# Moving the block products from the second batch to the first, in a two-branch sequence layer

## The chip, the cores and the metric

The kernel runs on one core of one Trainium2 chip. The metric is the device time of one execution in microseconds (us). The core has a matrix engine (TensorE, PE in the profile, with its weight loads as PEld), VectorE (DVE), ScalarE (ACT), GpSimd (POOL) and SyncE (SP), which here only issues DMAs. SBUF is the on-chip memory that all of them read; PSUM holds what TensorE writes.

## What is computed

One layer is applied to two batches (1024 positions, 1024 channels each) with the same weights. All data is float32. Cut to what matters:

```python
xn = rmsnorm(x, g_pre)
p = xn @ w_in
fv, fg, hv, hg, mg = jnp.split(p, [1024, 2048, 5120, 6144], axis=-1)

fz = jnp.fft.fftn(fv.reshape(B, L, 4, 256), axes=(1, 3), norm="ortho").real
y_f = (fz.reshape(B, L, 1024) * jax.nn.silu(fg)) @ w_fourier_out

hv = short_conv(hv, w_short)              # width 3 over the sequence
v, x1, x2 = jnp.split(hv, 3, axis=-1)
kf = hyena_filters(...)                   # same for both batches
z = v
for n, gate in enumerate((x1, x2)):
    z = gate * long_conv(z, kf[:, n], hyena_d[n])
y_h = (z * jax.nn.silu(hg)) @ w_hyena_out

g_f, g_h = jnp.split(jax.nn.sigmoid(mg + b_merge), 2, axis=-1)
out = (g_f * y_f + g_h * y_h) @ w_out
return x + rmsnorm(out, g_post)
```

The code numbers the in-projection's sections of 1024 columns, the Fourier input left out: 0 is fg, 1 to 3 are v, x1 and x2 ahead of the short convolution, 4 is hg, 5 and 6 are the two merge gates. A section has eight column tiles of 128 channels; with seven sections that is 56 tiles for each batch.

## The kernel before

To keep float32 accuracy, every large product is made three times over: each operand is split into a rounded high part and a low rest (`split`, L167: ScalarE rounds, another engine subtracts), and TensorE adds high x high, high x low and low x high (`mm3`, L467). A plain column tile (`inproj`, L836) is 8 row tiles x 3 x 2 halves of 512 positions, 48 matmuls of 512 columns. The split of its weights (wh and wl, from wr) has its subtraction on POOL.

A pair of column tiles can also be made by products of 2 x 2 blocks (`times`, L1101, used in `phase_gates`): seven products of block sums in place of eight, 84 matmuls in place of 96. This needs sums of row blocks (`sums`, L1110: xsum, th and tl), made once for a batch, and sums of weight blocks for each pair (`prepare`, L1129: wraw, wsum and their splits).

The stages follow each other: `phase_fourier` (both batches' norm and Fourier branch, stored in DRAM), `phase_main`, `phase_gates`, `phase_out` (output products). `phase_main` first makes the 16 filter spectra (2 orders x 8 channel tiles): taps, sums of absolute values (acc), butterflies (xp, xm, b) and a small transform (pXf), stored as kt. Beside them TensorE works on plain tiles of the first batch (`spill_gate`, L873). Then `branches` (L1030) runs 32 convolution steps, for each batch 2 orders x 8 channel tiles. A step transposes folded inputs (`conv_front`: eo, tph, xt), makes a butterfly (b, split into bh and bl), transforms (pX), multiplies by the spectrum (t, Y, split into yh and yl), transforms back (pT) and gates the result (`gate`). The steps of the two orders alternate, and the front of a step is issued ahead of the back of the one before. Beside the steps, `conv` (L863) makes the tile of v, x1 or x2 that a step needs: a plain in-projection, then three taps read from PSUM, one on ScalarE and two on VectorE. The first batch also stores its split weights in DRAM (d_w), and the second reads them there. The rows of the batch in work (xh and xl) are loaded and split by `load_x` (L823), ahead of each batch.

The tile framework assigns buffers and lets each instruction wait for its operands. It orders the instructions of every engine ahead of time; each engine then works through its own list in that order.

What the second batch gets before the change: its 24 tiles of v, x1 and x2 plain, 10 gate tiles plain near the end of the convolutions (`PLAIN`, L1116), and its other 22 gate tiles as 11 pairs of block products in `phase_gates`. The first batch's 56 tiles are all plain.

Of the kernel before, what the change touches and what calls it, by code (L numbers as in the profile page):

```python
# [9 lines left out]
F32 = mybir.dt.float32  # L10
# [127 lines left out]
NH = 6  # L138
NF = 8
# [6 lines left out]
GROUPS = [(0, (0, 1)), (2, (4, 5)), (1, (2, 3)), (3, (6, 7))]  # L146
KOFF = {0: 0, 1: 8, 2: 16, 3: 24}
# [13 lines left out]
class K:  # L161
# [34 lines left out]
    def setup(self, ctx):  # L196
# [28 lines left out]
        self.d_w = [[[dt(f"d_w{s}_{k}_{i}", [P, L]) for i in range(2)] for k in range(8)] for s in range(3)]  # L225
# [430 lines left out]
    def butterfly(self, ws, xp, xm):  # L656
# [77 lines left out]
    def filter_taps(self, n, ct, rates, ws):  # L734
# [8 lines left out]
        for m in range(4):  # L743
# [11 lines left out]
            if m:  # L755
                self.add("dve", accf, accf, ex)
# [14 lines left out]
    def filter_spectrum(self, n, ct, T, ws):  # L771
# [64 lines left out]
    def inproj(self, sec, mt, b=None):  # L836
# [3 lines left out]
        for q in range(2):  # L840
            s = slice(512 * q, 512 * q + 512)
            h = self.wp.tile([P, 4, P], F32R, tag="wh", name="wh", bufs=3)
            l = self.wp.tile([P, 4, P], F32R, tag="wl", name="wl", bufs=3)
            parts = [t.rearrange("p a b -> p (a b)") for t in (h, l)]
            kept = self.d_w[sec - 1][mt] if b is not None else None
            if b:
                for t, k in zip(parts, kept):
                    nc.sync.dma_start(t.bitcast(F32), k[:, s])
            else:
                r = self.wp.tile([P, 512], F32, tag="w", name="wr", bufs=2)  # L850
                nc.sync.dma_start(r, a["w_in"][sec, mt][:, s])
                self.split(*parts, r, "pool", "act")
                if kept:
                    for t, k in zip(parts, kept):
                        nc.gpsimd.dma_start(k[:, s], t.bitcast(F32))
# [7 lines left out]
    def conv(self, sec, ct, ws, name, b):  # L863
        nc = self.nc
        ps = self.inproj(sec, ct, b)
        out = ws.tile([P, L], F32, tag="u" if sec == 1 else "x", name=name, bufs=1 if sec == 1 else 4)
        w = lambda j: self.wsh[:, ((sec - 1) * 8 + ct) * 3 + j:((sec - 1) * 8 + ct) * 3 + j + 1]
        nc.scalar.activation(out, ps, AF.Copy, scale=w(1))
        self.stt("dve", out[:, 1:L], ps[:, 0:L - 1], w(0), out[:, 1:L])
        self.stt("dve", out[:, 0:L - 1], ps[:, 1:L], w(2), out[:, 0:L - 1])  # L870
        return out

    def spill_gate(self, b, sec, ct, ws):  # L873
# [4 lines left out]
        for n in range(2):  # L878
            s = slice(512 * n, 512 * n + 512)
            t = self.wp.tile([P, 512], F32, tag="gt", name="gt", bufs=3)  # L880
            if sec:
                nc.scalar.copy(t, ps[:, s])
            else:
                f = self.wp.tile([P, 512], F32, tag="gt", name="fz", bufs=3)
                nc.sync.dma_start(f, self.d_fz[b][ct][:, s])
                nc.scalar.activation(t, ps[:, s], AF.Silu)
                self.mul("dve", t, t, f)
            nc.sync.dma_start(self.d_g[b][sec][ct][:, s], t)


    def conv_front(self, u, ws):
# [4 lines left out]
        self.sub("dve", eo[:, 1], u4[:, :, P:2 * P], u4[:, :, P - 1::-1])  # L896
# [8 lines left out]
    def conv_back(self, n, ct, B, ws):  # L905
# [3 lines left out]
        for g, pairs in GROUPS:  # L909
# [25 lines left out]
            self.split(yh, yl, Y, "dve", "act")  # L935
# [47 lines left out]
    def phase_main(self, nct=8, nb=NB, nf=16):  # L983
        tc, nc, a = self.tc, self.nc, self.a
        with ExitStack() as es:
# [4 lines left out]
            with tc.issue_after(self.fz_stored.ins):  # L990
                self.load_x(0, range(4))
# [5 lines left out]
            with tc.issue_after(self.third[0].ins), tc.issue_after(self.third[1].ins):  # L997
                nc.scalar.copy(self.hid, hid)
                self.sub("dve", self.hid[64:128], hid[64:128], self.hid[64:128])
            taps = self.filter_taps(0, 0, self.filter_rates(0, 0, ws), ws)  # L1000
            self.load_x(0, range(4, 8))
# [3 lines left out]
            nc.gpsimd.tensor_copy(self.cfwd[:, 0, 0:1], self.xl[4][:, 0:1])  # L1005
            nc.gpsimd.dma_start(self.cfwd, a["c_fwd"])
            plain = [(5, c) for c in range(8)] + [(6, c) for c in range(8)] + [(4, c) for c in range(NH)]
            fill = sorted([((2 * c + 1) / len(plain), t) for c, t in enumerate(plain)]
                          + [((2 * c + 1) / max(NF, 1), (0, c)) for c in range(NF)])
            fill = [t for _, t in fill]  # L1010
            rates = self.filter_rates(1, 0, ws)
            for i in range(nf):
                nxt = self.filter_taps((i + 1) % 2, (i + 1) // 2, rates, ws) if i + 1 < nf else None
                self.filter_spectrum(i % 2, i // 2, taps, ws)
                if i + 2 < nf:
                    rates = self.filter_rates(i % 2, i // 2 + 1, ws, self.rounded)
# [13 lines left out]
    def branches(self, nb, nct, ws):  # L1030
# [10 lines left out]
        plain = list(self.PLAIN)  # L1041
# [576 lines left out]
```

## Time and profile before

| | us |
|---|---|
| median of 3 runs | 2398.74 |
| lowest and highest run | 2398.69, 2399.79 |
| span of the profiled execution | 2394.9 |
| last plain tile of the second batch ends | 1677.1 |
| block products (pg) run from there for about | 207.5 |

The span runs from the first to the last instruction of one profiled execution; the rest of the time lies around it. Durations of single instructions come from that execution. Busy time of an engine is the time in which at least one of its instructions ran; matmuls overlap in the pipeline, so the mean duration of one matmul (391 ns) is longer than the time between two. Idle time is put down to what ended it. A windows row gives, for a stretch of the span, its length and then the busy time and the count of instructions of each engine, the granted TensorE clock as a share of full speed, the share of DMA time and the DMA rate in GB/s.

### The profile page before, as it was taken

The numbers are of one execution on the slowest core, as the hardware profiler recorded it, in microseconds if no ns is written. First come the engines' busy times: TensorE is split into PE (matmuls) and PEld (weight loads), VectorE is DVE, ScalarE is ACT, GpSimd is POOL, SyncE is SP. The second block draws the span as 40 slices with busy tenths as digits, with TensorE's granted clock in tenths as the row PEclk, the third lists the DMA queues.
The fourth block names the chain that finished last, engine by engine and source line by source line (L and its number), as shares of the span: only waits on it lengthen the run. The fifth ranks groups of instructions, "written<-read, shape, count | busy, mean of one in ns | idle before, by whom it ended". The sixth has DMA issues, their size and how long they took to land.

```text
span 2394.9 us, 36369 instructions
## 1 busy us (share of the span) xinstructions
PE 2360.9 (99%) x12988; PEld 2053.6 (86%) x12988; DVE 1889.5 (79%) x3397; ACT 1084.2 (45%) x2063; POOL 461.6 (19%) x506
## 2 busy tenths in 40 slices
PE   6999999999999999999999999999999999999998
PEld 5998888888888888888888888888888888888887
DVE  7875787888879999999989999985555456665677
ACT  6654666677643333333322223333443445444444
POOL 3341222222232233230000000023000111112111
PEclk9999999999999999999999999999999999999999
DMA  8636655555665555545444444435544667776553
GB/s 264 219 129 220 204 169 165 171 171 159 204 215 177 172 170 187 176 145 203 150 131 133 137 150 133 143 121 198 165 160 141 211 215 259 251 259 213 166 166 132
DMA packets 221007, 428.33 MB, mean 179 GB/s; under 512 B 23254, under 2 KB 80952, under 8 KB 220570
## 3 DMA queue, kind: packets, MB, share of 16 engines
q1 hardware_dynamic: 193037, 333.03, 43.1%
q0 software_dynamic: 27568, 92.94, 11.5%
q8 instruction: 102, 1.67, 0.3%
q14 instruction: 79, 0.65, 0.1%
q10 hardware_dynamic: 221, 0.04, 0.0%
HBM read 290.12 MB, written 135.79 MB: 178 GB/s over the span
## 4 chain that ended last, share of the span: by engine, by line
PE 94%; DVE 2%; DMA 1%; ACT 1%; issue 1%; POOL 0%; DVEq 0%; ACTq 0%; POOLq 0%; SPq 0%
PE pin L193 41%; PE pg L193 8%; PE pyf L193 7%; PE pyh L193 7%; PE pX L193 7%; PE pT L193 7%; PE po L193 6%; PE pXf L193 3%; PE pfv L193 3%; PE pft L193 1%; PE tph L901 1%; DVE eo L180 0%; PE pQ L193 0%; DMA wr<-in_w_fo 0%; PE pse L193 0%
## 5 line engine op out<-in xcount | busy, mean ns | idle before, releaser
L193 PE MATMUL pin<-xh,wl 128*128 128x512 f32 x1440 | 563.2, 391 | 0.0
L193 PE MATMUL pin<-xl,wh 128*128 128x512 f32 x1440 | 562.8, 391 | 0.1
L193 PE MATMUL pin<-xh,wh 128*128 128x512 f32 x1440 | 561.9, 391 | 0.0
L180 POOL TENSOR_TENSOR wl<-wr,wh 128x512 fp32r<-128x512 f32 x132 | 227.6, 1725 | 1148.7 <-ACT wh L170 1125.4
L193 PEld LDWEIGHTS pin<-xl,wh 128*128 128x128 f32 x1440 | 271.0, 188 | 50.8 <-DVE xl L180 0.4
L193 PEld LDWEIGHTS pin<-xh,wh 128*128 128x128 f32 x1440 | 270.8, 188 | 51.0
L193 PEld LDWEIGHTS pin<-xh,wl 128*128 128x128 f32 x1440 | 271.0, 188 | 50.5
L170 ACT CAST wh<-wr 128x512 fp32r<-128x512 f32 x260 | 161.1, 620 | 333.6 <-PE pin L193 107.8
L180 DVE TENSOR_TENSOR t<-pX,k 128x1024 f32<-128x1024 f32 x128 | 155.6, 1216 | 9.8 <-PE pX L193 6.5
L193 PE MATMUL pX<-bh,cfwd 128*128 128x256 f32 x768 | 162.3, 289 | 0.0
L180 DVE TENSOR_TENSOR wl<-wr,wh 128x512 fp32r<-128x512 f32 x128 | 87.9, 688 | 91.5 <-ACT wh L170 91.5
L193 PE MATMUL pyf<-sf,wh 128*128 128x512 f32 x512 | 157.7, 389 | 0.0
L193 PE MATMUL pyh<-sh,wh 128*128 128x512 f32 x512 | 157.4, 389 | 0.0
L193 PE MATMUL pT<-cinv,yh 128*128 128x256 f32 x768 | 145.3, 284 | 0.0
L193 PEld LDWEIGHTS pT<-cinv,yh 128*128 128x128 f32 x768 | 123.2, 190 | 6.8
L170 ACT CAST bh<-b 128x512 fp32r<-128x512 f32 x144 | 89.1, 620 | 87.3 <-DVE b L180 50.6
L193 PEld LDWEIGHTS pX<-bh,cfwd 128*128 128x128 f32 x768 | 126.4, 190 | 2.2
L193 PEld LDWEIGHTS pyf<-sf,wh 128*128 128x128 f32 x512 | 96.1, 188 | 20.0
L193 PEld LDWEIGHTS pyh<-sh,wh 128*128 128x128 f32 x512 | 96.1, 188 | 20.0
L193 PE MATMUL pT<-cinv,yl 128*128 128x256 f32 x384 | 109.0, 284 | 0.0
L193 PE MATMUL pX<-bl,cfwd 128*128 128x256 f32 x384 | 108.9, 284 | 0.0
L170 ACT CAST yh<-y 128x512 fp32r<-128x512 f32 x96 | 59.4, 619 | 100.9 <-DVE y L180 98.0
(384 smaller groups left out, 5340.6 us busy)
## 6 DMA issues: line engine op xcount, KB each, us to landing
k<-d_k SPq DMA_DIRECT2D x128, 512.0 KB, 4.1
wr<-in_w_in SPq DMA_DIRECT2D x132, 256.0 KB, 3.2
d_g<-gt SPq DMA_DIRECT2D x124, 256.0 KB, 2.6
d_k<-kt SPq DMA_DIRECT2D x128, 128.0 KB, 2.2
d_k<-kt SPq DMA_DIRECT2D x64, 256.0 KB, 2.3
wr<-in_w_fo POOLq DMA_DIRECT2D x64, 256.0 KB, 4.0
g<-d_g SPq DMA_DIRECT2D x64, 256.0 KB, 4.2
wr<-in_w_ho POOLq DMA_DIRECT2D x64, 256.0 KB, 3.9
```

Source lines behind the costliest of these rows:

```text
L170: self.rounded = nc.scalar.copy(h, src)
L180: return e.tensor_tensor(out, a, b, op=op)
L193: return self.nc.tensor.matmul(out, lhsT, rhs, start=start, stop=stop, skip_group_check=shared)
L901: nc.tensor.transpose(tp[:, q * P:(q + 1) * P], eo[:, e, q], self.ident)
```

## The change

The two batches swap their treatment. A new stage `phase_products` stands ahead of `phase_main` and makes the whole in-projection of the first batch: four tiles plain (`FIRST`), the other 52 as 26 pairs of block products (`JOBS`). The tiles of v, x1 and x2 get their taps there, read from SBUF, and are stored (d_v); hg is stored behind its SiLU. `phase_gates` is gone, and so are the stored split weights (d_w).

`phase_main` now loads the second batch's rows ahead of the filters, and all 56 tiles of that batch are plain: 16 beside the filters (`FILL`), 17 beside the first batch's convolutions (`SIDE`, eight of them tiles of v, x1 and x2, listed in `AHEAD`, which are stored in d_v), 16 where the second batch's steps need them, and 7 near the end (`LAST`). The first batch's steps load v, x1 and x2 from DRAM. The product with SiLU(hg) is now made in the convolution step for both batches.

Several subtractions, additions and products move from VectorE to POOL: the low parts of b and y in the convolutions and filters, the sum of absolute taps, the odd folds of the filters and of the convolution inputs, the product with SiLU(hg), and two of the splits of a block product's weights. Two copies of the butterfly become one. Filters and convolutions are given a higher priority in the ordering than the plain tiles beside them. The first operands of `phase_out` go to buffers of their own and wait for the last convolution instead of the last block product.

```diff
+OFF = 1000
...
-        def split(g, b):
+        def split(g, b, eng="pool"):
...
-            self.split(h, l, b, "dve", "act")
+            self.split(h, l, b, eng, "act")
...
-        self.sub("dve", b2[:, 2], xp[:, 1, 3], xp[:, 1, 1])
-        self.sub("dve", b2[:, 3], xp[:, 1, 0], xp[:, 1, 2])
+        self.sub("dve", b2[:, 2:4], xp[:, 1, 3::-3], xp[:, 1, 1:3])
...
-                self.add("dve", accf, accf, ex)
+                self.add("pool", accf, accf, ex)
...
-            self.sub("dve", O[:, 2 * h:2 * h + 2], t[:, :, 0], t[:, :, 1])
+            self.sub("pool", O[:, 2 * h:2 * h + 2], t[:, :, 0], t[:, :, 1])
...
-        self.sub("dve", eo[:, 1], u4[:, :, P:2 * P], u4[:, :, P - 1::-1])
+        self.sub("pool", eo[:, 1], u4[:, :, P:2 * P], u4[:, :, P - 1::-1])
...
-            self.split(yh, yl, Y, "dve", "act")
+            self.split(yh, yl, Y, "pool", "act")
...
+    def conv(self, sec, ct, ws, name, b, tag=None):
+
+        tag = tag or ("u" if sec == 1 else "x")
+        out = ws.tile([P, L], F32, tag=tag, name=name, bufs=1 if tag == "u" else 4)
+        if b == 0 or (sec, ct) in self.AHEAD and name != "ahead":
+            self.nc.sync.dma_start(out, self.d_v[b][sec][ct])
+        else:
+            self.taps(out, self.inproj(sec, ct), sec, ct)
         return out
+
+    def beside(self, sec, c, ws):
+
+        if sec in (1, 2, 3):
+            out = self.conv(sec, c, ws, "ahead", 1, "u")
+            self.nc.sync.dma_start(self.d_v[1][sec][c], out)
+        else:
+            self.spill_gate(1, sec, c, ws)
...
-            with tc.issue_after(self.fz_stored.ins):
-                self.load_x(0, range(4))
+            self.load_x(1, range(4))
...
+            self.load_x(1, range(4, 8))
+            fill = self.FILL
...
+                with tc.high_priority(OFF):
+                    nxt = self.filter_taps((i + 1) % 2, (i + 1) // 2, rates, ws) if i + 1 < nf else None
+                    self.filter_spectrum(i % 2, i // 2, taps, ws)
...
-                    self.spill_gate(0, sec, c, ws)
+                    self.spill_gate(1, sec, c, ws)
...
+            if b == 0 and i:
+                for _ in range(len(side) - 15 + i if i > 13 or len(side) > 16 - i and i > 8 else 1):
+                    self.beside(*side.pop(0), ws)
...
+                    self.mul("pool", X[i][:, s], X[i][:, s], g)
...
-                if i + 2 < len(steps) and steps[i + 2][0] != steps[i + 1][0]:
-                    self.load_x(steps[i + 2][0])
-            y = self.conv_back(n, c, B, ws)
+            with tc.high_priority(OFF):
+                y = self.conv_back(n, c, B, ws)
...
-    PLAIN = [(5, 0), (5, 1), (6, 0), (6, 1), (5, 2), (5, 3), (6, 2), (6, 3), (5, 4), (5, 5)]
-
-    def phase_gates(self):
+    FIRST = [(5, 0), (5, 1), (5, 2), (5, 3)]
+    JOBS = ([(5, c) for c in (4, 6)] + [(s, c) for c in (0, 2, 4, 6) for s in (1, 4, 2, 0, 3)]
+            + [(6, c) for c in (0, 2, 4, 6)])
+    FILL = [(5, c) for c in range(8)] + [(6, c) for c in range(8)]
+    AHEAD = [(1, 0), (2, 0), (3, 0), (3, 1), (3, 2), (3, 3), (3, 4), (3, 6)]
+    SIDE = [(4, 0), (1, 0), (4, 1), (2, 0), (4, 2), (3, 0), (4, 3), (3, 2), (4, 4), (3, 4), (4, 5), (3, 6), (4, 6), (3, 1), (4, 7), (0, 0), (3, 3)]
+    LAST = [(0, c) for c in range(1, 8)]
+
+    def phase_products(self):
...
-                parts("s4", gw, ("s4h", "s4l"), s[:, 3], 1)
-                parts("22", gw, ("a2h", "a2l"), r[:, 3], 1)
+                parts("s4", gw, ("s4h", "s4l"), s[:, 3], 1, "pool")
+                parts("22", gw, ("a2h", "a2l"), r[:, 3], 1, "pool")
...
+            with tc.high_priority(600):
+                for k in range(4):
+                    if k == 2:
+                        A = prepare(*jobs[0])
...
+                if sec in (1, 2, 3):
+                    V[c, n] = True
+                    if (c, 1 - n) in V:
+                        o = xp.tile([P, L], F32, tag=f"xl{2 + c % 2}", name="tapped", bufs=1)
+                        self.taps(o, V[c], sec, c)
+                        nc.sync.dma_start(self.d_v[b][sec][c], o)
...
-            with tc.issue_after(self.copied.ins):
+            with tc.issue_after(self.ended.ins):
                 S = {(0, "f"): [rounded(operand(0, "f", k)) for k in range(8)]}
...
         k.open_x(ctx)
+        k.phase_products()
         k.phase_main()
-        k.phase_gates()
         k.phase_out()
```

More of the change, by code (lines that the diff above doesn't have):

```diff
@@ L135, in _tables @@
     return t
-NH = 6
-NF = 8
 IOFF = {}
@@ L840, in inproj @@
         for q in range(2):
[L841 to L855, printed above, removed]
+            h, l = self.plain_weights(sec, mt, q)
             for n in range(2):
@@ L1040, in branches @@
             steps.append((b, 1, nct - 1))
-        plain = list(self.PLAIN)
+        side, last = list(self.SIDE), list(self.LAST)
         Z, X, G = {}, {}, {}
@@ L1067, in close @@
             if i in G:
[L1068 to L1069 removed]
+                for q, g in enumerate(G.pop(i)):
                     s = slice(512 * q, 512 * q + 512)
[L1071 to L1074 removed]
+                    self.mul("pool", X[i][:, s], X[i][:, s], g)
         B = front(0)
@@ L1093, in branches @@
             nc.sync.dma_start(self.d_sh[b][c], z)
-            if b == 0 and NF <= c:
-                self.spill_gate(0, 0, c, ws)
-        with tc.issue_after(self.ended.ins):
-            for sec, c in plain:
-                self.spill_gate(1, sec, c, ws)
     def times(self, p, A, B, first):
```

189 lines of the change are left out of this document (108 added, 81 removed).

## The prediction

> **What bounds the kernel now.** I read the engine totals first, then the windows by stage, then the chain of waits at the seams between stages.
>
> ```profile
> PE 2360.9 (99%) x12988; PEld 2053.6 (86%) x12988; DVE 1889.5 (79%) x3397; ACT 1084.2 (45%) x2063; POOL 461.6 (19%) x506
> DVE  7875787888879999999989999985555456665677
> ```
>
> TensorE is busy throughout, and VectorE is at nine tenths or more in the slices of the convolutions. The stages show what that means. The columns are window, length, then busy time and count of PE, PEld, DVE, ACT and POOL.
>
> ```profile
> 203.00:684.00 481.00, 479.25 (x2620) 416.85 (x2619) 388.38 (x874) 321.86 (x680) 116.90 (x87) 1.00 0.57 181
> 684.00:1183.90 499.90, 498.66 (x2957) 441.82 (x2956) 470.59 (x749) 178.40 (x314) 125.52 (x127) 1.00 0.54 174
> 1183.90:1623.40 439.50, 439.50 (x2642) 391.36 (x2642) 401.30 (x665) 131.04 (x240) 24.46 (x13) 1.00 0.43 138
> 1677.10:1884.60 207.50, 207.05 (x914) 170.98 (x913) 117.25 (x167) 82.98 (x141) 12.18 (x23) 1.00 0.48 159
> ```
>
> These are the filters, the first batch's convolutions, the second's, and the block products. Each is bound by TensorE: it has no gap although VectorE is busy 94% of the first convolution window (470.59 of 499.90). So a VectorE at 94% does not yet cost TensorE anything in this program. The same three windows, for the plain in-projection alone:
>
> ```profile
> 203.00:684.00 481.00, 364.33 (x1547) 285.96 (x1547) 5.11 (x4) 35.25 (x62) 1.00 0.57 181
> 684.00:1183.90 499.90, 331.15 (x1364) 249.27 (x1364) 66.15 (x52) 31.13 (x30) 1.00 0.54 174
> 1183.90:1623.40 439.50, 284.72 (x1166) 212.44 (x1166) 51.03 (x40) 27.70 (x30) 1.00 0.43 138
> ```
>
> Matmul records overlap, so their price comes from the chain of waits, where TensorE runs unbroken:
>
> ```profile
> 1095.94 5.53 DMA xl<-d_x
> 1623.36 53.75 PE pin L193 x237
> 1677.11 184.82 PE pg L193 x815
> ```
>
> 53.75/237 and 184.82/815 are both 0.2268 us for one 512-column matmul. The first row is the one real stall in the middle: TensorE waits for the second batch's rows.
>
> **The change on TensorE.** A plain column tile is 48 such matmuls, 10.89 us, so a pair is 21.77 us. A pair by block products is 7 x 12 = 84 matmuls, 19.05 us. Before, 90 tiles are plain (4320 matmuls) and 11 pairs (924) are products. After, 60 tiles are plain (four of them in front of the products) and 26 pairs are products. Fifteen pairs more at 2.72 us each take 40.8 us off TensorE. The second batch's rows are now loaded once, before the filters, so the 5.53 us stall goes too, and its like returns at a seam (below). TensorE's own gain is thus 46.3 us, if it stays the bound.
>
> In the changed program's own order of TensorE instructions 960 plain matmuls of the second batch stand up to the end of the filters, 815 to the end of the first batch's convolutions, 810 to the end of the second's and 103 behind them: 2688, or 56 tiles. So TensorE needs, by the rows above: filters 481.0 - (1547 - 960) x 0.2268 = 348 us; first batch 499.9 - (1364 - 815) x 0.2268 - 5.5 = 370 us; second batch 439.5 - (1166 - 810) x 0.2268 = 359 us, and 23 us of plain matmuls behind it.
>
> **The products stage.** It grows from 11 pairs to 26 behind four plain tiles, about 539 us in all. VectorE was busy 117.25 of 207.50 us there, 57%. A pair of a convolution section adds four tap operations of 1.28 us (rows below): 5.1 us in 19.05, which brings VectorE to some 80%; two splits per pair leave it for POOL. I cost the stage at TensorE's time, as in the window of before. Without that cover each such pair would lose a few us.
>
> **VectorE and POOL beside the filters and convolutions.** With 34 plain tiles fewer to run beside them, the same filters and convolutions must be finished in less time, so the change moves VectorE work to POOL. The moved groups:
>
> ```profile
> L180 DVE TENSOR_TENSOR bl<-b,bh 128x512 fp32r<-128x512 f32 x144 | 98.7, 691 | 4.6 <-ACT bh L170 4.5
> L180 DVE TENSOR_TENSOR yl<-y,yh 128x512 fp32r<-128x512 f32 x96 | 67.5, 703 | 1.5 <-ACT yh L170 1.4
> L180 DVE TENSOR_TENSOR acc<-acc,ex 128x512 f32<-128x512 f32 x48 | 33.8, 705 | 2.7 <-ACT ex L754 2.7
> L180 DVE TENSOR_TENSOR fO<-T 128x512 f32<-128x512 f32 x32 | 20.6, 684 | 0.0
> L180 DVE TENSOR_TENSOR eo<-x 128x512 f32<-128x512 f32 x32 | 23.1, 762 | 0.1
> L180 DVE TENSOR_TENSOR eo<-v 128x512 f32<-128x512 f32 x32 | 20.7, 687 | 2.8 <-PE tph L901 2.8
> L180 DVE TENSOR_TENSOR x<-x,sg 128x512 f32<-128x512 f32 x16 | 10.4, 680 | 0.0
> L176 DVE SCALAR_TENSOR_TENSOR x<-pin,wsh,x 128x1023 f32<-128x1023 f32 x64 | 81.6, 1275 | 11.2 <-ACT x L868 11.2
> L180 POOL TENSOR_TENSOR wl<-wr,wh 128x512 fp32r<-128x512 f32 x132 | 227.6, 1725 | 1148.7 <-ACT wh L170 1125.4 <-PE pin L193 17.8 <-PE pXf L193 5.5
> L180 POOL TENSOR_TENSOR wl<-wr,wh x132: 1273/1304/4288, 175.8 to 1663.1; 128x512 fp32r<-128x512 f32 x132
> ```
>
> A moved operation of 0.69 us frees about 0.61 us, because neighbouring VectorE records overlap by 0.08 (two of 0.41 us start 0.34 apart in the timeline below). POOL pays 1.28 us for it at least (the minimum and median of the last row), 1.73 on average with its waits. The timelines say what the waits are:
>
> ```profile
> 643.46 1.29 POOL L180 TENSOR_TENSOR wl<-wr,wh 128x512 fp32r<-128x512 f32 x1 [5.36 <-ACT wh L170]
> 643.51 1.86 DVE L180 TENSOR_TENSOR b<-bs 128x256 f32<-128x256 f32 x2
> 711.07 0.41 DVE L180 TENSOR_TENSOR b<-bs,xt 128x256 f32<-128x256 f32 x1
> 711.25 2.05 POOL L180 TENSOR_TENSOR wl<-wr,wh 128x512 fp32r<-128x512 f32 x1 [5.47 <-ACT wh L170]
> 711.41 0.41 DVE L180 TENSOR_TENSOR b<-xt,bs 128x256 f32<-128x256 f32 x1
> 712.08 1.21 DVE L180 TENSOR_TENSOR t<-pX,k 128x1024 f32<-128x1024 f32 x1
> 713.32 0.69 DVE L180 TENSOR_TENSOR y<-t 128x512 f32<-128x512 f32 x1
> 377.31 3.33 POOL L180 TENSOR_TENSOR wl<-wr,wh 128x512 fp32r<-128x512 f32 x1 [4.01 <-ACT wh L170]
> ```
>
> At 643 POOL came first, and two VectorE additions of two SBUF operands, normally 0.75 us together, took 1.86. At 711 VectorE came first with such additions, POOL took 0.77 us longer than its 1.28, and the product with a PSUM operand ran beside it undisturbed. At 377 POOL waited 2 us. The two engines exclude each other for operations with two SBUF operands. The mean cost to VectorE: its groups between 203 and 1677 us exceed their own median durations by 38.9 us in all, over 129 POOL operations, 0.30 us each. The first and the fourth of those groups by size, with the median of the first (the undisturbed duration of the second is the 0.41 us above):
>
> ```profile
> L180 DVE TENSOR_TENSOR y<-t 128x512 f32<-128x512 f32 x128 | 90.8, 709 | 1.6 <-PE pT L193 1.2
> L180 DVE TENSOR_TENSOR y<-t x128: 673/684/1525, 708.9 to 1615.5; 128x512 f32<-128x512 f32 x128
> L180 DVE TENSOR_TENSOR b<-bs,xm 128x256 f32<-128x256 f32 x32 | 14.5, 490 | 0.0
> ```
>
> Now VectorE by stage, from its window before. Filters: 388.4, less 128 moved (48 bl, 48 acc, 32 fO) x 0.61 = 78, less 21 of old delay (71 weight splits on POOL x 0.30): 289 us. First batch: 470.6, less 128 moved (48 bl, 48 yl, 16 eo, 16 gate products) x 0.61 = 78, less 36 of 52 taps x 1.2 = 43 (only the eight tiles made ahead have taps here), less 10 for the row splits, less 26 of old delay: 314 us. Second batch: 401.3, less 112 moved x 0.61 = 68, less 8 of 40 taps, 10, less 4 of delay: 319 us. The old delays go by the weight splits on POOL in the same windows (last counts), the row splits by the last line:
>
> ```profile
> 203.00:684.00 481.00, 201.35 (x516) 97.05 (x516) 0.00 (x0) 107.33 (x71) 1.00 0.57 181
> 684.00:1183.90 499.90, 177.95 (x455) 85.68 (x455) 0.00 (x0) 104.74 (x86) 1.00 0.54 174
> 1183.90:1623.40 439.50, 152.35 (x389) 73.03 (x388) 0.00 (x0) 24.46 (x13) 1.00 0.43 138
> ...
> L180 DVE TENSOR_TENSOR xl<-xl,xh 128x1024 fp32r<-128x1024 f32 x8 | 9.7, 1217 | 2.2 <-ACT xh L170 2.2
> ```
>
> POOL operations are then 128 + 2 x 20 weight splits = 168, 128 + 34 = 162, and 128 + 38 = 166 (the second batch's gate products are on POOL too). At 0.30 us each they add 50, 49 and 50: 339 against TensorE's 348, 363 against 370, 369 against 359. The break-even delay is 0.35, 0.35 and 0.24 us per operation. So VectorE comes to 97 to 103% of TensorE: 10 us over in the second batch, and no slack elsewhere. For running that tight I add 12 us, between 0 (what 94% cost before) and 43 (what a delay of 0.40 would cost: 8 + 9 + 26). The delay itself is bounded by 0, where POOL only works while VectorE reads PSUM, and the whole 1.28; I take the measured mean, since the operations and their neighbours are of the same kinds.
>
> On this the Trainium skill has a rule that speaks against the change: "SBUF — State Buffer", section "SBUF: two separate sides", calls the shared pair of ports an exclusive lock, held for a whole instruction, in which the loser fully blocks. By the Trainium skill's rule, taken to its bound that VectorE always stands while POOL works, the time is rival 3's; the trace agrees in kind (1.86 us for 0.75) and not in amount (0.30 of 1.28 us).
>
> **The seams.** Fourier to products: VectorE has about 20 us behind its last Fourier operation (an estimate by size from 1.22 us for 1024 columns: four splits of 2048 columns, two groups of row sums and the first pair's weights), TensorE 80 plain and 24 product matmuls, 23.6 us, ahead of the first use: 2 us, at most 10. Products to filters: the second batch's last four row tiles cannot be loaded before the last products let go; the same wait was 5.53 us before, with 48 + 12 matmuls now in front: 3 us, 0 to 6. Convolutions to output: 103 matmuls, 23 us, cover eight loads and splits; before, weight loads of 6.24 us were covered here: 3 us, 0 to 6.
>
> ```profile
> 1865.47 6.24 DMA wr<-in_w_fo
> ```
>
> **The sum.** Span 2394.9, less 40.8, less 5.5, plus 10 overload, plus 12, plus 8 at the seams: 2378.6; with the 3.8 us between this span and the runs' median (2398.74), **2382 us**.
>
> **Rivals.** (1) The exclusion decides; slower. Place: the three stages beside filters and convolutions. With POOL at 496 operations instead of 129, delays per operation grow past the break-even. At 0.40 us the overload is 43 instead of 10, at 0.50 it is 93: 2415 to 2465, about 2425. It decides from about 0.37 on, where overload and the 12 us have eaten the 46.3 with the seams. For: the second batch is over already, and splits that TensorE waits for take 1.3 to 3.3 us where they took 0.69. Against: a POOL that always has work waiting starts when VectorE turns to PSUM, where it costs nothing. (2) TensorE stays the bound everywhere, delay at 0.26 or less: 2382 - 10 - 12 = 2360. For: 94% cost nothing. Against: no slack in any stage. (3) Full blocking, every POOL operation stops VectorE for 1.28 us: 289 + 215, 314 + 207 and 319 + 212 against 348, 370 and 359 is 479 us over: about 2850. For: the row at 643. Against: the row at 711, where the PSUM product ran on. (4) Gains and losses meet within 5 us of before.
>
> **How the numbers follow.** Forecast 0.42, and its own range is 2366 to 2394; rival 2 0.14; rival 4 0.08; rival 1 0.33; rival 3 0.03. Range 2357 to 2435. Beyond 0.2% (4.8 us, about what a measurement can tell from no change): faster 0.56, same 0.08, slower 0.36.
>
> **What would show it.** Right: about 5064 512-column matmuls in plain and product groups; the products stage near 539 us without gaps; VectorE at 95% or more of the three later stages; POOL 70 to 85% busy there, its means at 1.7 to 1.9 us; TensorE gaps of a few us at three seams. Wrong: gaps on TensorE all through the convolutions, waiting for low parts made on POOL (yl, bl), or VectorE groups of two SBUF operands more than 0.1 us above 0.69 on average; or gaps within the products stage.

## The result, and the profile after

The changed kernel takes 2635.4 us (median of 4 runs, 2634.8 to 2641.0) beside 2398.7 us of the kernel before on the same chip: a ratio of 1.099, interval 1.098 to 1.101. It is slower by 237 us. The forecast of 2382 us was wrong, and the range of 2357 to 2435 did not hold the time.

First the engine totals of the profile after, and its row of VectorE in 40 slices of the span:

```profile
PE 2411.4 (91%) x12808; PEld 2075.6 (79%) x12808; DVE 2034.1 (77%) x3097; ACT 1135.7 (43%) x2167; POOL 1021.7 (39%) x863
DVE  7865565665538999987999998899999846665687
```

TensorE has 180 matmuls fewer than before and is busy for 50 us more, yet 91% of the span instead of 99%. The stages tell where. These are windows of the kernel after: products, filters, first batch's convolutions, second batch's; the columns are those of the windows above.

```profile
208.00:770.00 562.00, 553.52 (x2431) 456.33 (x2430) 320.08 (x379) 233.86 (x357) 122.25 (x117) 0.99 0.39 134
770.00:1204.00 434.00, 369.54 (x1977) 320.12 (x1976) 382.47 (x678) 265.14 (x599) 257.35 (x175) 0.92 0.48 152
1204.00:1659.00 455.00, 396.93 (x2372) 350.44 (x2371) 416.91 (x555) 143.73 (x276) 240.99 (x163) 0.95 0.50 158
1659.00:2100.00 441.00, 386.77 (x2318) 343.12 (x2317) 417.03 (x550) 132.65 (x254) 229.76 (x158) 0.95 0.40 128
```

In the last three VectorE is the busier engine: 88, 92 and 95% of the window, and TensorE is busy for 85, 87 and 88%. Together they last 1330 us for 1077 us of TensorE's need. Of the 253 us over it, 177 are time in which TensorE does nothing (64.5 + 58.1 + 54.2, length less busy), and 76 are busy time beyond that need (1153 less 1077, at granted clocks of 0.92 to 0.95). By the view of TensorE's waits in these three stages some 138 us of the 177 are waits for results of VectorE, 31 for those of ScalarE and 7 for those of POOL. Two of its rows (us in total, times, longest):

```profile
PE pX L192 <- DVE b L179: 31.7, 18, 6.8
PE pn L761 <- DVE acc L179: 24.2, 9, 5.5
```

The VectorE groups that were shown before, and the groups now on POOL (busy, mean ns of one, idle before):

```profile
L179 DVE TENSOR_TENSOR y<-t 128x512 f32<-128x512 f32 x128 | 114.2, 892 | 15.9 <-PE pT L192 12.5 <-POOL yl L179 0.4
L179 DVE TENSOR_TENSOR b<-bs,xm 128x256 f32<-128x256 f32 x32 | 17.8, 595 | 0.0
L179 POOL TENSOR_TENSOR bl<-b,bh 128x512 fp32r<-128x512 f32 x144 | 204.3, 1423 | 131.2 <-ACT bh L169 122.0 <-issue 5.4 <-PE pin L192 2.2
L179 POOL TENSOR_TENSOR wl<-wr,wh 128x512 fp32r<-128x512 f32 x120 | 181.7, 1515 | 155.1 <-ACT wh L169 147.0 <-ACT yh L169 4.6 <-DMA cfw<-in_c_fw 1.8
L179 POOL TENSOR_TENSOR yl<-y,yh 128x512 fp32r<-128x512 f32 x96 | 147.7, 1539 | 203.4 <-ACT yh L169 183.8 <-PE pT L192 13.1 <-PE pin L192 6.5
```

VectorE's operations with two SBUF operands became longer (709 to 892 ns, 490 to 595), and POOL's became shorter (the splits of weights from 1725 to 1515 ns). One place in the timeline after (start, length, operation, count, idle before):

```profile
1318.36 2.29 POOL L179 TENSOR_TENSOR yl<-y,yh 128x512 fp32r<-128x512 f32 x1 [1.73 <-ACT yh L169]
1319.76 1.51 DVE L179 TENSOR_TENSOR b<-xt,bs 128x256 f32<-128x256 f32 x2
1321.19 0.75 DVE L179 TENSOR_TENSOR b<-bs,xt 128x256 f32<-128x256 f32 x2
```

The low part of y runs on POOL while VectorE makes b for the next step; two additions that took 0.75 us together where nothing disturbed them take 1.51, and POOL's operation of 1.28 us takes 2.29.

### The profile page after: what moved, and what is told of

Same layout as the page of the kernel before. It is cut to its first block, busy times and chain, and to the rows that moved or that the text cites. A ratio compares the mean times of both kernels' runs of the same rounds, so it can differ in the third digit from the quotient of the medians.

```text
span 2639.2 us, 36543 instructions
## 1 busy us (share of the span) xinstructions
PE 2411.4 (91%) x12808; PEld 2075.6 (79%) x12808; DVE 2034.1 (77%) x3097; ACT 1135.7 (43%) x2167; POOL 1021.7 (39%) x863
## 3 DMA queue, kind: packets, MB, share of 16 engines
q8 instruction: 101, 1.65, 0.3%
## 5 line engine op out<-in xcount | busy, mean ns | idle before, releaser
L192 PE MATMUL pin<-xh,wh 128*128 128x512 f32 x896 | 360.9, 404 | 36.4 <-DVE ahead L175 11.4
L192 PE MATMUL pin<-xl,wh 128*128 128x512 f32 x896 | 359.0, 401 | 0.0
L192 PE MATMUL pin<-xh,wl 128*128 128x512 f32 x896 | 358.4, 401 | 0.0
L179 POOL TENSOR_TENSOR bl<-b,bh 128x512 fp32r<-128x512 f32 x144 | 204.3, 1423 | 131.2 <-ACT bh L169 122.0
L179 POOL TENSOR_TENSOR wl<-wr,wh 128x512 fp32r<-128x512 f32 x120 | 181.7, 1515 | 155.1 <-ACT wh L169 147.0
L192 PEld LDWEIGHTS pin<-xh,wh 128*128 128x128 f32 x896 | 174.4, 195 | 72.5 <-ACT gt L896 12.0
L179 POOL TENSOR_TENSOR yl<-y,yh 128x512 fp32r<-128x512 f32 x96 | 147.7, 1539 | 203.4 <-ACT yh L169 183.8
L192 PEld LDWEIGHTS pin<-xl,wh 128*128 128x128 f32 x896 | 174.3, 195 | 33.3
L192 PEld LDWEIGHTS pin<-xh,wl 128*128 128x128 f32 x896 | 173.9, 194 | 33.6
L179 DVE TENSOR_TENSOR t<-pX,k 128x1024 f32<-128x1024 f32 x128 | 155.6, 1216 | 12.7 <-DMA k<-d_k 5.6
L192 PE MATMUL pg<-gxh,wh 128*128 128x512 f32 x376 | 128.6, 393 | 0.7 <-DVE gxh L179 0.7
```

The source lines that it names most:

```text
L179: return e.tensor_tensor(out, a, b, op=op)
L192: return self.nc.tensor.matmul(out, lhsT, rhs, start=start, stop=stop, skip_group_check=shared)
```

## The experiments

Fourteen kernels ran. In the short diffs a plus is the experiment's line. The first measures the disputed costs by themselves.

**micro**: only phases of 128x512 additions and subtractions (VectorE in A, POOL in B, both in C to F, with VectorE's operand in SBUF or in PSUM), then bursts of 40 matmuls after growing idle time.

```diff
+        phase("A", "s" * N, 0)
+        phase("B", "", N)
+        phase("C", "s" * N, N)
+        phase("D", "p" * N, N)
+        phase("E", "sp" * N, N)
+        phase("F", "sssp" * N, N)
```

> Only the measured pieces; it computes nothing of the layer. VectorE additions and POOL subtractions of 512 columns: 24 of VectorE with two SBUF operands alone (A), 24 of POOL alone (B), both together (C), VectorE with one PSUM operand beside POOL (D), alternating (E), three with two SBUF operands for one with PSUM (F); then bursts of 40 matmuls behind idle times of growing length. Theory 1 (the two engines exclude each other for two SBUF operands): A about 0.60 us each, B 1.28 each, C the sum of both, about 45 us for 24 pairs, D no slower than B alone (31 us), E and F between. Rival 2 (each engine only waits for its own inputs): C as long as B, 31 us. For the bursts: after an idle time above some limit of 2 to 5 us matmuls start at 0.43 us instead of 0.227 for about 4 us, below it they do not.

Windows of the phases A to F; the third and the fifth busy time after the length are VectorE and POOL:

```profile
4.90:19.50 14.60, 0.80 (x1) 0.29 (x1) 14.50 (x24) 1.26 (x3) 0.00 (x0) 1.00 0.00 0
21.40:50.80 29.40, 0.80 (x1) 0.29 (x1) 0.00 (x0) 0.61 (x2) 29.32 (x24) 1.00 0.00 0
52.00:92.50 40.50, 0.80 (x1) 0.29 (x1) 38.04 (x25) 1.29 (x3) 39.55 (x24) 1.00 0.00 0
94.60:124.10 29.50, 0.80 (x1) 0.29 (x1) 14.56 (x25) 0.47 (x1) 29.35 (x24) 1.00 0.00 0
125.30:166.70 41.40, 0.80 (x1) 0.29 (x1) 39.73 (x48) 1.26 (x3) 39.28 (x24) 1.00 0.00 0
168.00:247.00 79.00, 0.80 (x1) 0.29 (x1) 78.81 (x97) 1.29 (x3) 39.98 (x24) 1.00 0.00 0
```

Alone, VectorE takes 14.5/24 = 0.60 us and POOL 1.22 for one. Against POOL the 24 two-operand additions take 38.0 us: (38.0 - 14.5)/24 = 0.98 us of delay for each POOL operation, and POOL's operations rise to 1.65. With an operand in PSUM neither is delayed (D). With every other addition reading PSUM the delay is (39.7 - 48 x 0.60)/24 = 0.45 us, with every fourth (78.8 - 96 x 0.60)/24 = 0.88. So the delay is no constant: it runs from 0 to 1 us with the share of two-SBUF work that VectorE has ready. The two engines do exclude each other, though not wholly: C takes 39.5 us, 4 less than the sum of 43.8 and 10 more than POOL alone (29.3).

**undo**: the six moved groups back on VectorE.

```diff
-        def split(g, b, eng="pool"):
+        def split(g, b, eng="dve"):
...
-                self.add("pool", accf, accf, ex)
+                self.add("dve", accf, accf, ex)
...
-            self.split(yh, yl, Y, "pool", "act")
+            self.split(yh, yl, Y, "dve", "act")
```

> The six groups of operations (low parts of b and y, sums of absolute taps, odd folds of filters and inputs, product with SiLU(hg)) are back on VectorE, all else is as in the changed kernel. Theory 1 (496 POOL operations cost VectorE 0.62 us each by exclusion): VectorE's own time goes to about 333, 395 and 388 us in filters, first and second batch, with little delay on top, against TensorE's 348, 370 and 359: the three stages become 350, 405 and 400 us, 2450 to 2500 us in all. Rival 2 (POOL is merely a slower engine in a chain, and TensorE waits for its results): 2390 to 2440, TensorE-bound again. Rival 3 (the ordering with priority starves TensorE of plain tiles): no change, 2600 to 2660.

2604.3 us, ratio 1.086 (1.083 to 1.089): 31 us less than the changed kernel, where theory 1 expected at least 135. Its windows of filters and convolutions show why:

```profile
771.00:1186.00 415.00, 364.85 (x1980) 322.12 (x1980) 359.14 (x810) 268.40 (x599) 83.94 (x43) 0.91 0.50 160
1186.00:1639.00 453.00, 399.86 (x2399) 357.36 (x2398) 419.26 (x684) 146.67 (x277) 52.30 (x34) 0.94 0.47 160
1639.00:2078.00 439.00, 404.42 (x2398) 361.19 (x2396) 420.91 (x680) 141.91 (x264) 69.28 (x39) 0.95 0.40 136
```

VectorE is nearly as busy as in the changed kernel: 1199 us in sum, against 1216. Some 130 operations a stage of 0.6 us came back, and as much delay went. A move to POOL neither helped nor hurt VectorE much, so taking it back could not bring what theory 1 expected. This fits rival 3's number (the order) too, so that was tried next.

**noprio** and **undo0**: no order put ahead.

```diff
-OFF = 1000
+OFF = 0
```

> Changed kernel with the offset of the order put ahead set from 1000 to 0, so filter taps, spectra, transforms and gates are no longer moved ahead of the products of the same step; every operation stays. Theory 1 (VectorE is the bound of filters and convolutions: busy 382, 417 and 417 us of 434, 455 and 441, its work unchanged by this): 2600 to 2660 us. Rival 2 (the order put ahead makes TensorE wait on chains that are not ready, with the products, which are ready, queued behind): 2560 us or less, and TensorE's gaps in the three stages (177 us in the changed kernel) under 120.

> Changed kernel with the six moved groups of operations back on VectorE, and the offset of the order put ahead 0 instead of 1000. Theory 1 (VectorE, busy 358, 419 and 421 us in the three stages with the offset at 1000, binds): 2580 to 2630 us, as with 1000 (2604). Rival 2 (order): 2540 us or less.

2632.5 us (ratio 1.098, 1.097 to 1.100) and 2599.5 us (1.084, 1.083 to 1.086), 3 and 5 us from the same kernels with the offset. VectorE's busy time stays at 1213 and 1200 us. TensorE's gaps in the three stages of noprio are 161 us, where rival 2 expected under 120. The order put ahead is not the cause.

**actlow**, **actlow2**, **nopool**, **nopool0**: VectorE's load lowered without a change to TensorE's work, by writing low parts on ScalarE: those of b and y; the same, in the convolutions twice over; those of the plain weights as well; and the last with the offset at 0.

```diff
+        if eng == "copy":
+            self.left = nc.scalar.copy(l, src)
...
-        def split(g, b, eng="pool"):
+        def split(g, b, eng="copy"):
...
-            self.split(yh, yl, Y, "pool", "act")
+            self.split(yh, yl, Y, "copy", "act")
```

> The low parts of b and y are made by ScalarE as a copy of the source in place of the difference (so the low parts are wrong numbers of the same shape); the other moves to POOL stay. It takes 240 of 496 operations from POOL and adds nothing to VectorE. Theory 1: VectorE loses about 0.6 us of delay for each of them, comes to 320 to 350 us a stage, TensorE is the bound again: 2370 to 2420 us. Rival 3 (ordering): 2550 to 2660. Both theory 1 and rival 2 (latency of the chain) gain here; the next run tells these two apart.

> As the run before, but in the convolutions ScalarE makes each such copy twice, so that a low part takes 1.24 us behind its high part, as long as it took POOL without waits, and no port that VectorE uses is held. Theory 1: within 25 us of the run before, 2370 to 2440 us. Rival 2 (latency of POOL in the chain): most of what the run before gained in the two convolution stages is lost again, 2500 to 2600 us.

> Changed kernel with the low parts of plain weights, of the convolutions' spectrum input and of their products written as copies on ScalarE instead of subtractions on POOL: the low parts are then wrong numbers of the same shape, and the three stages have about 100 fewer operations each on POOL. Theory 1 (VectorE's own work plus the delay by POOL's operations is the bound): VectorE's busy time falls to about 300, 335 and 335 us, under TensorE's need of 348, 370 and 359, so TensorE binds and the time is 2400 to 2435 us (2635 less the 253 us by which the three stages are longer than TensorE's need, plus 20 to 50 for seams). Rival 2 (order and latency, whatever VectorE's load): the stages stay at 390 us or more as with the copies for two of the three kinds, 2490 to 2520 us. Rival 3 (ScalarE, which gets about 100 copies of 0.62 us per stage more, binds): over 2520 us.

> The kernel with all three kinds of low parts as ScalarE copies (wrong numbers in them), and the offset of the order put ahead 0 instead of 1000. Theory 1: within 20 us of the same with 1000. Rival 2 (order): over 40 us faster than the same with 1000.

2514.2 us (1.049), 2506.1 (1.045), 2463.0 (1.027) and 2484.7 (1.037). In the convolutions the doubled copies cost nothing (8 us less), so a low part that is ready 0.62 us later there does not lengthen them. The copies for two kinds gain 121 us and for the third another 51. Theory 1 missed both in size (2370 to 2420, 2400 to 2435), and nopool's stages of 391, 388 and 380 us are close to rival 2's 390; but of all kernels with the changed one's TensorE work only these come down by more than 36 us, and the more VectorE is relieved the further. With the copies for all three kinds the kernel with the offset of 1000 is the faster one by 22 us, against rival 2 (theory 1 had allowed for 20). The windows of nopool:

```profile
770.00:1161.00 391.00, 358.56 (x1988) 314.58 (x1987) 322.06 (x683) 304.93 (x689) 137.48 (x87) 0.95 0.54 170
1161.00:1549.00 388.00, 373.08 (x2363) 335.97 (x2362) 344.54 (x552) 207.71 (x405) 50.60 (x32) 0.99 0.55 186
1549.00:1929.00 380.00, 368.25 (x2330) 332.10 (x2329) 338.83 (x547) 199.68 (x382) 44.52 (x29) 0.99 0.44 148
```

Here TensorE is the busier engine again (1100 of 1159 us), though even with VectorE at 82 to 89% the three stages stay 82 us above TensorE's need. Some 32 us of the 82 are gaps in the filters, nearly all of them behind 1091 us, from where to the end of the stage no plain product is left; how much of the rest is latency of single chains was not tried.

**cut** and **aftercut**: the counter test. One of the three matmuls of each plain product is left out, in the kernel before and in the changed one.

```diff
-                    self.mm3(ps[:, s], (h[:, kk], l[:, kk]), (self.xh[k][:, s], self.xl[k][:, s]), k == 0, k == 7)
+                    self.mm(ps[:, s], h[:, kk], self.xh[k][:, s], k == 0, False)
+                    self.mm(ps[:, s], h[:, kk], self.xl[k][:, s], False, k == 7)
```

> The kernel before, with one of the three matmuls of each plain product left out (the one by the low part of the weight, so the plain products are rounded wrong); nothing is moved and no other order is asked for. TensorE's need falls by a third of the plain matmuls at 0.227 us: from 481, 495 and 444 us in filters, first and second batch's convolutions to about 364, 392 and 355, close to the changed kernel's 348, 370 and 359; VectorE's work stays at 388, 465 and 406 us busy. Theory 1 (with so little cover VectorE is the bound and TensorE waits on its chains): the three stages take 1335 to 1385 us of the 1420 before, 2295 to 2345 us in all. Rival 2 (it is the changed kernel's moves and order that make TensorE wait): 2071 to 2130 us, TensorE without gaps.

> The changed kernel with one of the three matmuls of each plain product left out (the one by the low part of the weight), 896 matmuls of 0.227 us, 203 us of TensorE's work, nearly all of it in the filters and convolutions. Theory 1 (there VectorE alone is the bound, TensorE's time counts for nothing): 2590 to 2635 us. Rival 2 (the two engines bind in turn, TensorE's work on the chain): 2450 to 2570 us. Rival 3 (TensorE binds): 2430 us or less.

2350.2 us (ratio 0.980, 0.978 to 0.982) and 2601.7 us (1.085, 1.083 to 1.087). Some 327 us less of TensorE's work (1440 of 4320 plain matmuls) make the kernel before 48 us faster, and 203 us less make the changed one 34 us faster. For cut this is 5 us above theory 1's range in all, with the three stages inside it (1379 us); aftercut is inside theory 1's range. With no operation moved, by this alone, the kernel before comes to look like the changed one: TensorE's gaps in the three stages are 176 us, beside 177. Here are the windows of filters, first and second batch in cut, with TensorE at 85, 89 and 88% and the clock below 1.

```profile
203.00:673.00 470.00, 398.81 (x2132) 346.30 (x2131) 397.70 (x869) 320.88 (x680) 125.48 (x96) 0.92 0.58 188
673.00:1154.00 481.00, 426.03 (x2480) 374.14 (x2479) 464.69 (x740) 176.24 (x312) 111.62 (x119) 0.95 0.58 194
1154.00:1582.00 428.00, 378.36 (x2277) 335.25 (x2276) 411.29 (x680) 133.87 (x247) 31.75 (x15) 0.95 0.37 126
```

And the same three in aftercut, where TensorE's busy time fell by 136 us, the length by 24 and VectorE's work by 18:

```profile
771.00:1201.00 430.00, 315.46 (x1651) 275.55 (x1650) 383.50 (x676) 261.62 (x594) 258.61 (x174) 0.84 0.48 154
1201.00:1654.00 453.00, 355.56 (x2143) 319.05 (x2142) 411.26 (x558) 146.86 (x280) 240.81 (x167) 0.88 0.49 162
1654.00:2077.00 423.00, 346.30 (x2084) 309.35 (x2082) 403.09 (x556) 141.84 (x265) 231.47 (x159) 0.92 0.45 144
```

**bmoves**: the kernel before with the six groups on POOL (the undo diff reversed).

> The kernel before, with the same six groups of operations moved from VectorE to POOL as in the change, and nothing else. Theory 1 (a move of a 0.6-us operation saves VectorE 0.6 us and costs it 0.55 to 0.65 us of delay, and TensorE's plain products cover the longer chains): VectorE's own time falls by about 75 us in each of the three stages and its delay grows by as much, time 2390 to 2420 us. Rival 2 (the moves lengthen the chains, and that alone costs): over 2440 us. Rival 3 (the moves free VectorE as they were meant to): VectorE busy 50 us or more less in the first batch's convolutions, and time within 2385 to 2400 us as TensorE binds.

2493.7 us, ratio 1.040 (1.039 to 1.041): a miss for theory 1, inside rival 2's range. VectorE's load is as expected hardly changed (1266 us busy in the three stages, 1260 before), but the cover was not enough. Windows of filters and first batch's convolutions in bmoves:

```profile
203.00:701.00 498.00, 459.91 (x2437) 396.18 (x2436) 397.85 (x731) 305.28 (x658) 286.31 (x194) 0.96 0.49 160
701.00:1259.00 558.00, 534.19 (x3038) 466.81 (x3037) 471.51 (x615) 183.87 (x326) 311.26 (x280) 0.98 0.50 166
```

In the filters TensorE stands for 38 us while VectorE stands for 100: neither is the bound, the chain is. One row of the view of TensorE's waits names more than half of it, the sum of absolute taps, whose additions now follow one another on POOL (median 1.34 us each, 0.68 on VectorE before):

```profile
PE pn L763 <- DVE acc L180: 20.6, 8, 4.0
```

In the first batch's convolutions TensorE waits another 24 us. So with plain tiles enough beside them the moves cost 95 us, with VectorE's busy time unchanged, which points at longer chains; where VectorE is the bound anyway (undo) they cost 31.

**plain8**, **plain6** and **plain8b**: the kernel before with a little more of what the change does, one or two pairs of the second batch's plain tiles made by block products; in plain8b the pair comes from beside the last two convolution steps and not from behind them. The diff is plain8's.

```diff
-    PLAIN = [(5, 0), (5, 1), (6, 0), (6, 1), (5, 2), (5, 3), (6, 2), (6, 3), (5, 4), (5, 5)]
+    PLAIN = [(6, 0), (6, 1), (5, 2), (5, 3), (6, 2), (6, 3), (5, 4), (5, 5)]
```

> The kernel before, with one pair of the second batch's plain tiles made by block products too (8 plain tiles left instead of 10). Theory 1 (TensorE without gaps as long as plain tiles cover VectorE's chains; the four tiles behind the last convolution cover more than its chain): 2.7 us less, 2392 to 2396 us. Rival 2 (the cover behind the last convolution is used up): 2400 to 2420 us.

> The kernel before, with two pairs of the second batch's plain tiles made by block products too (6 plain tiles left instead of 10, none behind the last convolution). Theory 1: 5.4 us of TensorE saved, but no cover is left between the last convolution and the first block product, whose operands VectorE makes: a gap of 10 to 30 us there, 2403 to 2425 us. Rival 2 (the cover isn't needed): 2390 to 2394 us.

> The kernel before, with one pair more by block products, this time taken from the four plain tiles behind which the last convolutions stand (2 of the 6 beside them), the four behind the last convolution left in place. Theory 1 (VectorE is busy 92 to 100% of the second batch's convolutions, so 22 us less of TensorE's work beside them turns to waiting): 2402 to 2418 us. Rival 2 (there is slack left): 2394 to 2397 us.

2410.6 us (1.005, 1.004 to 1.007), 2426.3 (1.012, 1.010 to 1.013) and 2408.2 (1.004, 1.003 to 1.005). Even one pair, from either place, is too many. plain8 fits its rival 2 and plain8b its theory 1; plain6 is 1 us above theory 1's range. TensorE in plain8, at the first sums of row blocks:

```profile
1664.19 0.49 PE L193 MATMUL pg<-th,s2h 128*128 128x512 f32 x1 [2.00 <-ACT th L170]
1666.52 0.80 PE L193 MATMUL pg<-tl,s2h 128*128 128x512 f32 x1 [1.83 <-DVE tl L180]
...
1673.02 0.80 PE L193 MATMUL pg<-th,s2h 128*128 128x512 f32 x1 [5.28 <-ACT th L170]
```

The two tiles gone were the cover under which ScalarE and VectorE prepare th and tl: the kernel before has no wait there, plain8 has 10.7 us (9.1 in these rows) with a granted clock of 0.89 behind them, and plain6 has 25.7. In plain8b the longest wait is in the last convolution (4.5 us in front of a pT). No version found here, with the whole computation, beats the kernel before.

## Why the prediction was wrong

The three stages of each kernel but the plain ones in one table: sums of the window rows. TensorE's need is worked out from the plain matmuls left, as in the prediction; in noprio, undo, undo0 and nopool0 the plain tiles behind the convolutions have moved among them.

| kernel | TensorE's need | VectorE busy | length | length less VectorE |
|---|---|---|---|---|
| before | 1420 | 1260 | 1420 | 160 |
| cut | 1111 | 1274 | 1379 | 105 |
| changed | 1077 | 1216 | 1330 | 114 |
| noprio | 1100 | 1213 | 1332 | 119 |
| undo | 1100 | 1199 | 1307 | 108 |
| undo0 | 1100 | 1200 | 1301 | 101 |
| aftercut | 897 | 1198 | 1306 | 108 |
| actlow | 1078 | 1074 | 1204 | 130 |
| actlow2 | 1079 | 1078 | 1197 | 119 |
| nopool | 1079 | 1005 | 1159 | 154 |
| nopool0 | 1100 | 1009 | 1185 | 176 |
| bmoves | 1420 | 1266 | 1516 | 250 |

Where VectorE is clearly busy for more than TensorE's need (cut, changed, noprio, undo, undo0, aftercut), the length is VectorE's busy time and 101 to 119 us, whatever TensorE has to do (897 to 1111). That is the bound that the change ran into, and it was near already: 1260 and 101 to 119 is 1361 to 1379, so the kernel before had only 40 to 60 us of TensorE's work to give away in these stages as a whole, and cut, which takes 309 out, gets 41. The change takes 343 out. At a single place even less can be too much, as plain8b shows. And bmoves shows a second cost that this rule does not cover: its stages are 96 us longer than the larger of the two loads.

The span by place, forecast and measured:

| | forecast | measured |
|---|---|---|
| ahead of the products | 203 | 208 |
| products with their first seam | 539 + 2 | 562 |
| filters and convolutions: TensorE's need, overload, tight running, seam | 1077 + 10 + 12 + 3 | 1330 |
| plain tiles behind, seam | 23 + 3 | 24 + 5 |
| output | 510 | 510 |

The first failed step is "At 0.30 us each they add 50, 49 and 50: 339 against TensorE's 348, 363 against 370, 369 against 359". VectorE's own work was about right: with each VectorE record counted at the tenth percentile of its kind (the duration that a tenth of them stay under), and the overlap of neighbouring records taken off, it is 913 us for the 922 forecast. The forecast's 71 and 86 weight splits on POOL were 64 and 45, the rest of these counts being DMA issues; with the right counts its own working gives 936. The delay was not right: what the records take beyond that percentile is 303 us over 491 POOL operations, 0.62 each (0.69 in the filters, 0.57 and 0.58 in the convolutions). VectorE came to 382, 417 and 417 us, 139 over TensorE's need instead of 10. That is 129 us of the miss.

Why 0.30 was too low has two parts. One is the base. The prediction took each group's median as undisturbed; with the tenth percentile the kernel before has 50 us of delay over 122 weight splits in the three stages, 0.41 each. At 0.40 the prediction's own working gives an overload of 43 us in place of 10. The other is who pays. In the kernel before POOL paid for much of the collisions itself: 1725 ns against its 1273 undisturbed, 0.45 us, beside VectorE's 0.41. In the changed kernel the three POOL groups stand at about 1.48 us, 0.21 over that, and VectorE pays 0.62. The sums, 0.86 and 0.83, are alike, but no fixed price follows: counted in the same way they are 0.72 in bmoves and 1.15 in undo, and 0.87 to 1.41 in the phases C, E and F of micro. What makes POOL come first more often after the change was not tried.

The consequence is that the moves were worth nothing. The Trainium skill says so of offloading between these two engines, "Perfetto Trace Analysis", section "Optimizing Scalar/DVE Operations": with the shared read port it "might not help". The runs agree, with a number: by the comparison above each moved operation saved VectorE 0.55 to 0.58 us and cost it 0.54 to 0.74 us of delay (undo beside the changed kernel, by stage).

The second failed step is "For running that tight I add 12 us". The premise, that a VectorE at 94% costs nothing, held in the kernel before because TensorE was the bound and had plain products ready in every wait. Once VectorE is the bound, it too has waits of its own, 114 us in the changed kernel, and TensorE's ready work cannot fill those. That is 99 us more than the 15 forecast with the seam. On TensorE the same time appears as gaps and, behind many of them, matmuls at half the rate. The delay by POOL alone does not explain the loss: with the six groups back on VectorE (undo) the stages still last 1307 us, and cut, with no operation moved, reaches the same bound.

The prediction also took a row of the chain for a stall. "The first row is the one real stall in the middle: TensorE waits for the second batch's rows" does not hold: in that stretch of the kernel before TensorE is busy throughout.

```profile
1095.90:1101.50 5.60, 5.60 (x32) 4.85 (x31) 5.60 (x8) 3.61 (x6) 0.00 (x0) 1.00 1.01 403
```

So nothing was to be won there: TensorE's own gain was about 41 us and not 46.3, and its need in the first batch's convolutions is 4 to 5 us more than the forecast and the rows of the table built on it (all but before, cut and bmoves) say.

The third failed step is small. The products were forecast with a seam of 2 us, "at most 10", and took 21 more than 541: 8.5 us of gaps, up to 8 at a granted clock of 0.93, both ahead of 320 us, and 3.4 us for 15 plain matmuls that came early. Timeline rows of the kernel after:

```profile
269.07 0.51 PE L192 MATMUL pg<-th,s2h 128*128 128x512 f32 x1 [2.07 <-ACT th L169]
272.13 0.80 PE L192 MATMUL pg<-tl,s2h 128*128 128x512 f32 x1 [2.55 <-DVE tl L179]
274.66 0.80 PE L192 MATMUL pg<-th,s2h 128*128 128x512 f32 x1 [1.31 <-ACT th L169]
```

The row sums (th, tl) are not ready when TensorE comes to them. From 320 us on the stage has no gap, as forecast.

Of the rivals the first had the mechanism and the place, at a price too small: its 0.40 to 0.50 us gave 2415 to 2465, since it counted the delay and not VectorE's own waits on top. Rival 3's full blocking (1.28) is excluded by micro's 0.98 at most and by the 0.62 here. Right were the counts (5064 plain and block matmuls), VectorE's own work, the output and the TensorE rate in the products. Of the signs named for "right", POOL's share of 70 to 85% (52 to 59% measured), its means of 1.7 to 1.9 us and VectorE's 95% or more (88, 92 and 95%) failed. The signs for "wrong" came in part: two-operand groups are more than 0.1 us longer and TensorE has gaps throughout, but these are mostly waits for VectorE's results and hardly for low parts from POOL (7 of 177 us).

## What to carry to other kernels

Work that keeps the busiest engine full may also be the cover of the second one: before taking it out, compare what is left with the busy time of the next engine in that stage plus its own idle time, here VectorE's 1260 us and 101 to 119 more, and expect nothing below that. Removing a third of such work for a trial (cut) tells this bound in one run, ahead of any restructuring. A move of two-operand SBUF work from VectorE to POOL should be priced by what both engines lose in a collision, and by the longer chain, not by the time that VectorE alone loses today.

## What the runs showed of the hardware

TensorE's clock falls after a short wait. Bursts of 40 matmuls in micro behind 1.34, 1.99, 3.28 and 3.93 us of idle time (in brackets):

```profile
261.00 9.38 PE L67 MATMUL gap<-r,w 128*128 128x512 f32 x40 [1.34 <-ACT r L75]
272.37 10.99 PE L67 MATMUL gap<-r,w 128*128 128x512 f32 x40 [1.99 <-ACT r L75]
300.27 10.98 PE L67 MATMUL gap<-r,w 128*128 128x512 f32 x40 [3.28 <-ACT r L75]
315.19 12.04 PE L67 MATMUL gap<-r,w 128*128 128x512 f32 x40 [3.93 <-ACT r L75]
```

Against the first burst those behind 1.99 and 3.28 us take 1.6 us more and that behind 3.93 us takes 2.7 more; four behind longer waits, of 4.6 to 7.8 us, take 1.9 to 2.9 more. One burst was measured for each length. In the changed kernel (timeline after) the matmuls behind such a wait start 0.43 us apart instead of 0.23:

```profile
1000.88 0.77 PE L761 MATMUL pn<-acc,ones 128*128 128x128 f32 x2 [5.53 <-DVE acc L179]
...
1003.15 0.63 PE L192 MATMUL pin<-xh,wl 128*128 128x512 f32 x1
1003.58 0.63 PE L192 MATMUL pin<-xh,wh 128*128 128x512 f32 x1
```

By the Trainium skill, "TensorE: Matmul & The Clock Gate", section "Part 1: The HAM clock gate (the "warmup" mystery)", TensorE drops to half its clock after an idle window of about 3.4 us and needs as long to come back. The halving agrees, and so does the time of recovery behind 1.99 and 3.28 us, where the granted clock is at half for 3.4 us; around the wait of 3.93 us it is at half for 6.8, and the wait that sufficed was shorter here, 1.99 us. In the changed kernel TensorE is busy for 123 us at half the clock in the three stages; at 0.43 in place of 0.23 us for a matmul that is an estimated 58 of the 76 us by which its busy time exceeds its need, though with VectorE as the bound only a part of it can have cost time.
